# Moving every operand of the float32r matmuls to one place modulo 512 bytes

## The chip, the cores and the metric

The kernel runs on one core of a Trainium2 chip. The metric is the device time of one launch in microseconds (us), taken as the median of several runs. A core has TensorE (PE in the profile, its loads of stationary operands as PEld), VectorE (DVE), ScalarE (ACT), GpSimd (POOL) and SyncE (SP), which work side by side on an on-chip memory of 128 partitions; TensorE writes its sums into a second, smaller memory, PSUM. An operand's address below is its byte offset inside a partition, the same in all 128, and its *place* is that address modulo 512.

## The reference

One layer of a hybrid decoder on 1024 tokens of width 2048, all in float32: an RMS norm, one input projection to 8200 columns, two recurrences on its parts, an output projection, a gated per-layer input, a last norm.

```python
u = rmsnorm(h, norm_w[l])
proj = einsum('bsd,dc->bsc', u, w_in[l])
...
h_a = mlstm_chunkwise(q_a, k_a, v_a, i_pre, f_pre)
y_a = sigmoid(ml_o) * rmsnorm(h_a) * silu(ml_z)
h_b = hgrn2_chunkwise(q_b, k_b, logf_b, i_b)
y_b = rmsnorm(h_b) * silu(hg_g)
h = h + einsum('bsc,cd->bsd', concat([y_a, y_b]), w_out[l])
e = einsum('bsr,rd->bsd', p[l], w_pe[l])
gate = sigmoid(einsum('bsd,de->bse', rmsnorm(h, pe_norm_w[l]), w_pg[l]))
out = rmsnorm(h + gate * e, final_norm_w)
```

## The kernel before

The four large products (input projection, output projection, gate, per-layer input) are float32 products made of three float32r passes. Each operand is split into a rounded *high* part and the exact remainder, the *low* part (`split`, L113 to L115: a cast on ScalarE, then a subtraction on VectorE). The helper `mm3` then issues three matmuls into one PSUM bank: high by high (L242), high by low (L243), low by high (L244). A matmul has a *stationary* operand of 128x128, which a load (LDWEIGHTS in the trace) brings into the array, and a *moving* operand of 128 rows by 512, 264 or 256 columns that streams past it.

Tokens are handled in two halves of 512. First part, for each half: `prep_u` makes 16 split tiles `u` of the normed input; `proj_ch` (outputs `pj`) takes slices of the weights `hl` as stationary and `u` as moving operand, 512 columns wide; `proj_tok` (outputs `pt`) has it the other way round, `u` stationary and `hl` moving, 256 columns wide (264 in one block a half, the one that carries the gates). Between these stand the recurrences, whose matmuls are plain float32, apart from `col_sums` (L514, L515), which multiplies a stationary tile of ones, `ones_r`, by split products. Second part, for each half: output projection (outputs `po`, stationary `ys`, the split mixed heads; moving `hl_o`), then the gate (outputs `pg`, stationary `hnt`; moving `hl_g`) and the per-layer input (outputs `pe`, stationary `pp`; moving `hl_e`). All have 512 columns but the last token tile of all (`bg`), which has two groups of 256.

Weights come in pieces of 128x1024 float32, three pieces ahead, by DMAs on SP's queue into `raw` (pool `wpool`, three buffers) and are split into `hl`, also three buffers. A `hl` tile has two planes, high and low, of WP = 1056 columns each. The order of the instructions is made by a scheduler when the kernel is built; GpSimd writes `y` and `h` to DRAM and is otherwise nearly idle.

Where a tile lies in a partition follows from the order in which the pools are opened and from their sizes. Before, the runtime's DMA scratch (16,384 bytes) and 128 bytes of small constants come first, then `const`, `upool`, `stage`, `wpool`, `small`, `mix`; `tl` takes `mix`'s room in the second part. `upool` starts at 19,360 = 37 x 512 + 416, and a `u` tile has 4,096 bytes, so every `u` and `ys` plane has place 416. A `hl` buffer has 8,448 = 16.5 x 512 bytes and a plane 4,224 = 8.25 x 512, so places alternate between buffers.

| operand (pool) | place before | place after |
|---|---|---|
| `u`, `ys`, high and low (`upool`) | 416 | 128 |
| `hl`, high plane, three buffers | 288, 32, 288 | 128 |
| `hl`, low plane, three buffers | 416, 160, 416 | 128 |
| `hnt` and `pp` (`tl`) | 448 | 128 |
| `ones_r` | 96 | 128 |
| split products of `col_sums` (`mix`) | 448 | 128 |

In the 264-column block the slices of `hl` are 1,056 bytes apart, so there the place of the moving operand advances by 32 bytes from slice to slice, before and after.

Of the kernel before, what the change touches and what calls it, by code (L numbers as in the profile page):

```python
"""Hybrid decoder layer (mLSTM heads and HGRN2 heads side by side) on one core.

Tokens are handled in two halves. The projections run as float32 products split
into three float32r passes (each operand is the sum of a rounded part and an exact
remainder), channels on the output partitions, so that both recurrences find their
queries and keys transposed. The recurrences work in chunks of 128 tokens; HGRN2's
decays are formed as products over blocks of doubling size, so no factor exceeds one.
"""
# [9 lines left out]
F32R = mybir.dt.float32r  # L18
# [6 lines left out]
P = 128  # L25
# [6 lines left out]
AHEAD = 3  # L32
WP = 1056
BIG = 1e30
LEVELS = (4, 8, 16, 32, 64)
# [8 lines left out]
def hybrid_layer(ctx: ExitStack, tc, x, xT, pT, w_blk, w_v0, w_out, w_pg, w_pe, vec, gb, fnw,  # L44
                 ident_in, causal_in, lmask_in, out):
    nc = tc.nc
    PS = bass.MemoryType.PSUM

    const = ctx.enter_context(tc.tile_pool(name="const", bufs=1))
    upool = ctx.enter_context(tc.tile_pool(name="upool", bufs=17))  # L50
    stage = ctx.enter_context(tc.tile_pool(name="stage", bufs=3))
    wpool = ctx.enter_context(tc.tile_pool(name="wpool", bufs=3))
# [13 lines left out]

# [1 line left out]
    vec_sb = const.tile([P, V_END], F32, name="vec_sb")  # L68
# [10 lines left out]
    nc.vector.memset(ones, 1.0)  # L79
    ones_r = const.tile([P, P], F32R, name="ones_r")  # L80
    nc.scalar.copy(out=ones_r, in_=ones)

    # lower bound: softmax over the two rows, first row
    lb = const.tile([P, 8], F32, name="lb")
# [12 lines left out]

    # states carried between halves
    mcar = const.tile([4, 1], F32, name="mcar")
# [11 lines left out]

# [1 line left out]
    def split(dst_hi, dst_lo, src):  # L113
# [8 lines left out]

    # weights arrive as [P, 1024] slices in the order of use, some slices ahead
    w_order, w_tiles = [], []
# [15 lines left out]
    def next_piece(between=None):  # L140
        nm, src = w_order[len(w_tiles)]
        n = src.shape[1] * src.shape[2]
        raw = wpool.tile([P, WP], F32, tag="wraw", name=f"raw_{nm}")[:, 0:n]
        if nm in LATE:
            hl = [upool.tile([P, 2, HT], F32R, tag="u", name=f"hl_{nm}_{i}") for i in range(2)]
            nc.sync.dma_start(out=raw, in_=src.rearrange("p k c -> p (k c)"))
            for i in range(2):
                split(hl[i][:, 0], hl[i][:, 1], raw[:, i * 512:(i + 1) * 512])
            w_tiles.append((nm, hl))
            return  # L150
        hl = wpool.tile([P, 2, WP], F32R, tag="whl", name=f"hl_{nm}")[:, :, 0:n]
        parts = 4 if not w_tiles else 1
        for i in range(parts):
            k0, k1 = i * src.shape[1] // parts, (i + 1) * src.shape[1] // parts
            sl = slice(k0 * src.shape[2], k1 * src.shape[2])
            nc.sync.dma_start(out=raw[:, sl], in_=src[:, k0:k1].rearrange("p k c -> p (k c)"))
            if between is not None:
                between(i)
            split(hl[:, 0, sl], hl[:, 1, sl], raw[:, sl])
        w_tiles.append((nm, hl))  # L160

    def load_piece(name):
        """the next slice of weights, split: [P, 2, n]"""
        while len(w_tiles) < len(w_order) and (len(w_tiles) < AHEAD or w_order[len(w_tiles) - AHEAD][0] != name):
            next_piece()
        return dict(w_tiles[-AHEAD - 4:])[name]

    def prep_stats(half):
        """1 / rms of the tokens: as columns [P, chunk] and as a row on every partition"""
        ss = small.tile([P, NC, 4], F32, tag="ssx", name=f"ssx{half}")  # L170
# [27 lines left out]
    def prep_u(half):  # L198
        """x^T times the norm weight, split; 1 / rms is applied to the projections"""
        us = []  # L200
# [45 lines left out]
    def proj_ch(half, us, b):  # L246
        """two column tiles of the block, channels on partitions: two banks [P, 512]"""
        ps = [psj(f"pj{half}_{b}_{i}") for i in range(2)]
        for pc in range(4):
            hl = load_piece(f"{half}_{b}_{pc}")  # L250
            for kk in range(4):
                k = pc * 4 + kk
                for i in range(2):
                    sl = slice(kk * 256 + i * P, kk * 256 + (i + 1) * P)
                    mm3(ps[i], hl[:, 0, sl], hl[:, 1, sl], us[k][:, 0], us[k][:, 1], k == 0, k == KT - 1)
        return ps

    def proj_tok(half, us, b, n=256):
        """the block with tokens on partitions: four banks [P, n]"""
        ps = [psj(f"pt{half}_{b}_{i}") for i in range(NC)]  # L260
# [10 lines left out]

# [1 line left out]
    def gates(half, pv, rc):  # L273
        """pv: banks with the gates' input and forget parts in columns 256-259 and 260-263"""
        gp = small.tile([P, NC, 8], F32, tag="gp", name=f"gp{half}")
# [13 lines left out]
        nc.scalar.activation(out=fp, in_=prow[1][0:4, :], func=AF.Identity, bias=gb_sb[:, 1:2])  # L289
        # log sigmoid(f) = min(f, 0) - log1p(exp(-|f|)), log1p(e) = 2 atanh(e / (2 + e))  # L290
        nc.vector.scalar_tensor_tensor(out=t1, in0=fp, scalar=-1.0, in1=fp, op0=ALU.mult, op1=ALU.max)
# [6 lines left out]
        for n in (15, 13, 11, 9, 7, 5, 3):  # L298
# [3 lines left out]
        nc.vector.scalar_tensor_tensor(out=fp, in0=t3, scalar=-2.0, in1=fp, op0=ALU.mult, op1=ALU.add)  # L302
        # cumulative log forget inside a chunk, running maximum
        nc.vector.tensor_tensor_scan(out=b_, data0=rst, data1=fp, initial=0.0, op0=ALU.mult, op1=ALU.add)
# [17 lines left out]
                                in1=alast.unsqueeze(2).broadcast_to([4, NC, P]), op=ALU.add)  # L322
        # columns: beta, floor exp(-m), state weight
        stk = mix.tile([P, HT], F32, tag="y", bufs=2, name=f"stk{half}")[0:68]
# [8 lines left out]
        nc.vector.tensor_copy(out=cols, in_=pc[:, 0:NC * 68].rearrange("p (c r) -> p c r", r=68))  # L333
        # rows, broadcast over partitions through DRAM
        rows = tc.dram_tile([4, 2, HT], F32, name=f"rows{half}")
# [4 lines left out]

# [1 line left out]
    def mlstm_unit(half, us, hd, rs, gc):  # L342
        n = f"{half}_{hd}"
# [57 lines left out]

        # decays and weighted scores, keys on partitions
        dq = mix.tile([P, 2 * NC, P], F32, tag="at", bufs=1, name=f"dq{n}")
# [58 lines left out]

# [1 line left out]
    def hgrn_unit(half, us, pr, rs):  # L464
# [35 lines left out]

        # scores within a chunk: the diagonal, then pairs of blocks of doubling size
        qf = q.rearrange("p a b -> p (a b)")
# [4 lines left out]
        def col_sums(prod, name):  # L507
            """sums over the partitions of [P, 512] products, on every partition"""
            tag = ("kh", "sg")[spl[0] % 2]
# [7 lines left out]

        # pairs inside a block of four tokens: elementwise products, summed over the state dimension
        ff = f.rearrange("p a b -> p (a b)")
# [41 lines left out]
        toff = HT + 256  # L561
        # pairs of blocks of doubling size
        for li, s in enumerate(LEVELS):
# [24 lines left out]
            toff += nblk  # L588
        # T: product of the forget gates over each chunk
        kh = mix.tile([P, H2, P], F32, tag="kh", bufs=1, name=f"hkh{n}")  # L590
# [54 lines left out]

# [1 line left out]
    rs = None  # L647
# [13 lines left out]

# [1 line left out]
    tl = ctx.enter_context(tc.tile_pool(name="tl", bufs=1, reuse_waits="tile"))  # L663
    for half in range(2):
# [53 lines left out]
        def gate_block(cb, ts_, pref):  # L718
            """gate and per-layer input for the token tiles ts_ of one block of 512 columns"""
            cs = slice(cb * 512, (cb + 1) * 512)  # L720
            wpe = load_piece(f"{pref}e{half}_{cb}")
            pe_sb = {}
            for t in ts_:
# [5 lines left out]
                pe_sb[t] = pe  # L729
            # the last tile of all comes in two groups of columns, to shorten what follows its products  # L730
            units = []
# [138 lines left out]
```

## Time and profile before

| | |
|---|---|
| time, median of 3 runs | 2429.19 us (2429.04 to 2430.67) |
| span of the profiled execution | 2427.2 us |
| instructions | 30,855 |
| TensorE busy | 2410.4 us, 99% of the span |
| VectorE busy | 1166.3 us, 48% |
| ScalarE busy | 767.8 us, 32% |
| DMA | 287.57 MB, mean 118 GB/s |

The span goes from the first to the last instruction of one execution that the profiler recorded; that execution has no other time of its own, and its span is 2.0 us under the median of the runs. A matmul's recorded duration runs to the end of its pipeline, and that end is modelled, so that consecutive matmuls overlap in a list by time. What a matmul costs is the *step*: the distance from its start to the start of the next one.

### The profile page before, as it was taken

The numbers are of one execution on the slowest core, as the hardware profiler recorded it, in microseconds if no ns is written. First come the engines' busy times: TensorE is split into PE (matmuls) and PEld (weight loads), VectorE is DVE, ScalarE is ACT, GpSimd is POOL, SyncE is SP. The second block draws the span as 40 slices with busy tenths as digits, with TensorE's granted clock in tenths as the row PEclk, the third lists the DMA queues.
The fourth block names the chain that finished last, engine by engine and source line by source line (L and its number), as shares of the span: only waits on it lengthen the run. The fifth ranks groups of instructions, "written<-read, shape, count | busy, mean of one in ns | idle before, by whom it ended". The sixth has DMA issues, their size and how long they took to land.

```text
span 2427.2 us, 30855 instructions
## 1 busy us (share of the span) xinstructions
PE 2410.4 (99%) x12700; PEld 2044.1 (84%) x12700; DVE 1166.3 (48%) x1657; ACT 767.8 (32%) x1211; POOL 66.3 (3%) x96
## 2 busy tenths in 40 slices
PE   8999999999999999999999999999999999999998
PEld 7888889888888888888888888888888888888887
DVE  6655344355564847344246364565423444332336
ACT  6433232223222424223222222242322334332225
POOL 0000000000000000000000000000000000000000
PEclk9999999999999999999999999999999999999999
DMA  8433332222222423333332222243444446444336
GB/s 315 136 97 103 94 100 94 91 78 93 79 87 81 156 78 105 96 108 101 94 107 87 87 79 89 78 150 122 135 130 127 132 146 222 135 154 130 117 114 212
DMA packets 93461, 287.57 MB, mean 118 GB/s; under 512 B 10872, under 2 KB 11640, under 8 KB 93320
## 3 DMA queue, kind: packets, MB, share of 16 engines
q1 hardware_dynamic: 88200, 268.82, 35.0%
q0 software_dynamic: 5120, 16.78, 1.8%
q8 instruction: 99, 1.62, 0.3%
q14 instruction: 42, 0.34, 0.0%
HBM read 260.36 MB, written 25.20 MB: 118 GB/s over the span
## 4 chain that ended last, share of the span: by engine, by line
PE 98%; DMA 0%; issue 0%; DVE 0%; ACT 0%; SPq 0%; POOL 0%; POOLq 0%; ACTq 0%; DVEq 0%
PE pj L244 15%; PE pj L243 15%; PE pj L242 15%; PE pg L242 5%; PE pt L242 5%; PE pg L244 5%; PE pt L244 5%; PE pg L243 5%; PE po L242 5%; PE pt L243 5%; PE po L244 5%; PE po L243 5%; PE pl L570 2%; PE pe L242 1%; PE pe L244 1%; PE pe L243 1%
## 5 line engine op out<-in xcount | busy, mean ns | idle before, releaser
L242 PE MATMUL pj<-u,hl 128*128 128x512 f32 x1536 | 608.0, 399 | 5.9 <-ACT hl L114 5.9
L244 PE MATMUL pj<-u,hl 128*128 128x512 f32 x1536 | 611.3, 399 | 0.0
L243 PE MATMUL pj<-u,hl 128*128 128x512 f32 x1536 | 610.8, 398 | 0.2 <-DVE u L230 0.2
L114 ACT CAST hl<-raw 128x1024 fp32r<-128x1024 f32 (+2 forms) x259 | 269.2, 1040 | 863.1 <-PE pj L244 449.1
L115 DVE TENSOR_TENSOR hl<-raw,hl 128x1024 fp32r<-128x1024 f32 (+2 forms) x259 | 313.5, 1211 | 402.4 <-ACT hl L114 402.2
L242 PEld LDWEIGHTS pj<-u,hl 128*128 128x128 f32 x1536 | 289.1, 188 | 72.6 <-ACT hl L114 5.9
L243 PEld LDWEIGHTS pj<-u,hl 128*128 128x128 f32 x1536 | 289.4, 188 | 70.0 <-DVE u L230 1.1
L244 PEld LDWEIGHTS pj<-u,hl 128*128 128x128 f32 x1536 | 289.1, 188 | 66.7 <-issue 0.2
L242 PE MATMUL pt<-hl,u 128*128 128x256 f32 (+1 forms) x1024 | 291.1, 285 | 0.4 <-DVE raw L357 0.4
L244 PE MATMUL pt<-hl,u 128*128 128x256 f32 (+1 forms) x1024 | 290.2, 285 | 0.0
L243 PE MATMUL pt<-hl,u 128*128 128x256 f32 (+1 forms) x1024 | 288.8, 283 | 0.0
L242 PE MATMUL po<-hl_o,ys 128*128 128x512 f32 x512 | 202.1, 395 | 0.0
L244 PE MATMUL po<-hl_o,ys 128*128 128x512 f32 x512 | 200.3, 392 | 0.0
L243 PE MATMUL po<-hl_o,ys 128*128 128x512 f32 x512 | 199.8, 390 | 0.0
L242 PEld LDWEIGHTS pt<-hl,u 128*128 128x128 f32 x1024 | 193.7, 189 | 2.2 <-issue 1.1
L243 PEld LDWEIGHTS pt<-hl,u 128*128 128x128 f32 x1024 | 194.0, 189 | 1.3
L244 PEld LDWEIGHTS pt<-hl,u 128*128 128x128 f32 x1024 | 192.4, 188 | 0.9 <-issue 0.2
L242 PE MATMUL pg<-hl_g,hnt 128*128 128x512 f32 x448 | 177.9, 397 | 0.0
L244 PE MATMUL pg<-hl_g,hnt 128*128 128x512 f32 x448 | 177.9, 397 | 0.0
L243 PE MATMUL pg<-hl_g,hnt 128*128 128x512 f32 x448 | 177.1, 395 | 0.0
L115 DVE TENSOR_TENSOR hl_o<-raw_o,hl_o 128x1024 fp32r<-128x1024 f32 x64 | 78.4, 1225 | 161.9 <-ACT hl_o L114 161.9
L115 DVE TENSOR_TENSOR hl_g<-raw_g,hl_g 128x1024 fp32r<-128x1024 f32 x56 | 68.6, 1225 | 174.5 <-ACT hl_g L114 174.5
(264 smaller groups left out, 2642.9 us busy)
## 6 DMA issues: line engine op xcount, KB each, us to landing
raw<-in_w_blk_dram SPq DMA_DIRECT2D x247, 512.0 KB, 3.9
raw_o<-in_w_out_dram SPq DMA_DIRECT2D x64, 512.0 KB, 3.6
raw_g<-in_w_pg_dram SPq DMA_DIRECT2D x56, 512.0 KB, 3.7
yr<-y SPq DMA_DIRECT2D x32, 256.0 KB, 4.0
xr<-in_x_dram SPq DMA_DIRECT2D x32, 256.0 KB, 5.7
h<-ht POOLq DMA_DIRECT2D x32, 256.0 KB, 6.3
hr<-h SPq DMA_DIRECT2D x32, 256.0 KB, 3.6
out_dram<-h SPq DMA_DIRECT2D x32, 256.0 KB, 3.5
```

What stands on the lines that cost most here:

```text
L114: nc.scalar.copy(out=dst_hi, in_=src)
L115: nc.vector.tensor_tensor(out=dst_lo, in0=src, in1=dst_hi.bitcast(F32), op=ALU.subtract)
L242: nc.tensor.matmul(ps, lhsT=ah, rhs=bh, start=first, stop=False)
L243: nc.tensor.matmul(ps, lhsT=ah, rhs=bl, start=False, stop=False)
L244: nc.tensor.matmul(ps, lhsT=al, rhs=bh, start=False, stop=last)
L570: nc.tensor.matmul(pl[0:M, c * 64:(c + 1) * 64], lhsT=kf[:, c * P:c * P + M], rhs=qv[:, c * nb:(c + 1) * nb, 1, :], start=True, stop=True)
```

## The change

The diff without its removed comment lines and docstrings (line numbers behind the helpers grow by four):

```diff
+WH = 1152
...
-    const = ctx.enter_context(tc.tile_pool(name="const", bufs=1))
     upool = ctx.enter_context(tc.tile_pool(name="upool", bufs=17))
+    hlpool = ctx.enter_context(tc.tile_pool(name="hlpool", bufs=3))
+    orpool = ctx.enter_context(tc.tile_pool(name="orpool", bufs=1))
     stage = ctx.enter_context(tc.tile_pool(name="stage", bufs=3))
+    const = ctx.enter_context(tc.tile_pool(name="const", bufs=1))
     wpool = ctx.enter_context(tc.tile_pool(name="wpool", bufs=3))
...
-    ones_r = const.tile([P, P], F32R, name="ones_r")
+    ones_r = orpool.tile([P, P + 112], F32R, name="ones_r")[:, 0:P]
...
-        hl = wpool.tile([P, 2, WP], F32R, tag="whl", name=f"hl_{nm}")[:, :, 0:n]
+        hl = hlpool.tile([P, 2, WH], F32R, tag="whl", name=f"hl_{nm}")[:, :, 0:n]
...
-    nc = _bacc.Bacc("TRN2", target_bir_lowering=False, num_devices=1)
+    nc = _bacc.Bacc("TRN2", target_bir_lowering=False, num_devices=1, dynamic_dma_scratch_size=8192)
```

`upool` comes first, behind a DMA scratch of half the size, and starts at 8,320 = 16 x 512 + 128. The split weights have a pool of their own right behind it, with planes of 1152 columns = 9 x 512 bytes. `ones_r` follows, with 112 columns of padding behind it that nothing reads; the padding sets where `mix`, and with it `tl`, begins: 129,152 = 252 x 512 + 128. The table above has the places that result. On every engine the built program has the same instructions on the same operands in the same order as before, and the same waits; only the addresses differ.

## Rows read from the trace of the kernel before

**Rows 1.** The page: busy time, share of the span and count by engine; the granted TensorE clock in 40 slices (tenths of full speed); the chain of work that ended last, by engine.

```profile
PE 2410.4 (99%) x12700; PEld 2044.1 (84%) x12700; DVE 1166.3 (48%) x1657; ACT 767.8 (32%) x1211; POOL 66.3 (3%) x96
...
PEclk9999999999999999999999999999999999999999
...
PE 98%; DMA 0%; issue 0%; DVE 0%; ACT 0%; SPq 0%; POOL 0%; POOLq 0%; ACTq 0%; DVEq 0%
```

**Rows 2.** What TensorE waited for: us in total, times, longest.

```profile
PE pj L242 <- ACT hl L114: 5.9, 1, 5.9
PE prow L282 <- DVE gp L277: 1.0, 1, 1.0
```

**Rows 3.** Groups of TensorE's instructions by line and shape: output and operands, rows and columns, count, busy us and mean ns of one, idle before.

```profile
L244 PE MATMUL pj<-u,hl 128*128 128x512 f32 x1536 | 611.3, 399 | 0.0
L243 PE MATMUL pj<-u,hl 128*128 128x512 f32 x1536 | 610.8, 398 | 0.2 <-DVE u L230 0.2
L242 PE MATMUL pj<-u,hl 128*128 128x512 f32 x1536 | 608.0, 399 | 5.9 <-ACT hl L114 5.9
L242 PE MATMUL pt<-hl,u 128*128 128x256 f32 x896 | 254.8, 285 | 0.0
...
L243 PE MATMUL pt<-hl,u 128*128 128x256 f32 x896 | 252.3, 282 | 0.0
L242 PE MATMUL po<-hl_o,ys 128*128 128x512 f32 x512 | 202.1, 395 | 0.0
L244 PE MATMUL po<-hl_o,ys 128*128 128x512 f32 x512 | 200.3, 392 | 0.0
L243 PE MATMUL po<-hl_o,ys 128*128 128x512 f32 x512 | 199.8, 390 | 0.0
L242 PE MATMUL pg<-hl_g,hnt 128*128 128x512 f32 x448 | 177.9, 397 | 0.0
L244 PE MATMUL pg<-hl_g,hnt 128*128 128x512 f32 x448 | 177.9, 397 | 0.0
L243 PE MATMUL pg<-hl_g,hnt 128*128 128x512 f32 x448 | 177.1, 395 | 0.0
...
L244 PE MATMUL pe<-hl_e,pp 128*128 128x512 f32 x56 | 22.2, 397 | 0.0
...
L244 PE MATMUL pg<-hl_ag,hnt 128*128 128x512 f32 x32 | 12.7, 397 | 0.0
...
L243 PE MATMUL pg<-hl_bg,hnt 128*128 128x512 f32 x16 | 6.3, 395 | 0.0
```

**Rows 4.** Instructions of TensorE in order of time in the input projection, `pj`: start us, duration us, line, operands. From the first row to the last are 12 steps.

```profile
799.65 0.40 PE L244 MATMUL pj<-u,hl 128*128 128x512 f32 x1
799.89 0.39 PE L242 MATMUL pj<-u,hl 128*128 128x512 f32 x1
800.12 0.40 PE L243 MATMUL pj<-u,hl 128*128 128x512 f32 x1
...
802.45 0.40 PE L244 MATMUL pj<-u,hl 128*128 128x512 f32 x1
```

**Rows 5.** The same in the output projection, `po`; 12 steps from the first row to the last.

```profile
1759.63 0.39 PE L244 MATMUL po<-hl_o,ys 128*128 128x512 f32 x1
...
1762.38 0.39 PE L244 MATMUL po<-hl_o,ys 128*128 128x512 f32 x1
```

**Rows 6.** The same in the gate, `pg`; 12 steps from the first row to the last.

```profile
1899.78 0.40 PE L244 MATMUL pg<-hl_g,hnt 128*128 128x512 f32 x1
...
1902.58 0.40 PE L244 MATMUL pg<-hl_g,hnt 128*128 128x512 f32 x1
```

**Rows 7.** The same in a block with 256 columns, `pt`; 24 steps from the first row to the last.

```profile
1181.91 0.28 PE L244 MATMUL pt<-hl,u 128*128 128x256 f32 x1
...
1184.80 0.28 PE L244 MATMUL pt<-hl,u 128*128 128x256 f32 x1
```

**Rows 8.** Matmuls and loads of stationary operands together, in order of time, in the output projection: the load that a matmul of one line needs carries that line.

```profile
1760.10 0.39 PE L243 MATMUL po<-hl_o,ys 128*128 128x512 f32 x1
1760.10 0.19 PEld L244 LDWEIGHTS po<-hl_o,ys 128*128 128x128 f32 x1
1760.32 0.39 PE L244 MATMUL po<-hl_o,ys 128*128 128x512 f32 x1
1760.32 0.19 PEld L242 LDWEIGHTS po<-hl_o,ys 128*128 128x128 f32 x1
```

**Rows 9.** Groups by line: the two instructions that split a piece of weights of the input projection (count, busy us and mean ns of one, idle before and what ended it).

```profile
L115 DVE TENSOR_TENSOR hl<-raw,hl 128x1024 fp32r<-128x1024 f32 (+2 forms) x259 | 313.5, 1211 | 402.4 <-ACT hl L114 402.2
...
L114 ACT CAST hl<-raw 128x1024 fp32r<-128x1024 f32 (+2 forms) x259 | 269.2, 1040 | 863.1 <-PE pj L244 449.1 <-PE pt L244 162.6 <-issue 84.4
```

**Rows 10.** DMA issues by line: queue, count, KB each, median us from issue to landing.

```profile
raw<-in_w_blk_dram SPq DMA_DIRECT2D x247, 512.0 KB, 3.9
...
h<-ht POOLq DMA_DIRECT2D x32, 256.0 KB, 6.3
...
y<-hy POOLq DMA_DIRECT2D x16, 256.0 KB, 3.2
```

More of the change, by code (lines that the diff above doesn't have):

```diff
@@ L47, in hybrid_layer @@
     PS = bass.MemoryType.PSUM
+    upool = ctx.enter_context(tc.tile_pool(name="upool", bufs=17))
+    hlpool = ctx.enter_context(tc.tile_pool(name="hlpool", bufs=3))
+    orpool = ctx.enter_context(tc.tile_pool(name="orpool", bufs=1))
+    stage = ctx.enter_context(tc.tile_pool(name="stage", bufs=3))
     const = ctx.enter_context(tc.tile_pool(name="const", bufs=1))
-    upool = ctx.enter_context(tc.tile_pool(name="upool", bufs=17))
-    stage = ctx.enter_context(tc.tile_pool(name="stage", bufs=3))
     wpool = ctx.enter_context(tc.tile_pool(name="wpool", bufs=3))
```

## The prediction

> **What bounds the kernel now.** I read the page first. TensorE is busy 99% of the span, the chain of work that ended last lies on it for 98%, and the granted clock stands in the top tenth in all 40 slices [rows 1]: the upper of its two levels, 2.4 GHz, throughout. The list of waits comes next, since a busy engine may hide short stalls: the longest is 5.9 us, at the start, and the next is 1.0 us [rows 2]. So no transfer, no split and no other engine sets the time; what a change can win or lose is the time that TensorE takes from one matmul to the next. The change moves no instruction, so only that step can differ.
>
> The third view is therefore TensorE's instructions in order of time, of which the reader is to take the distance between starts, not the durations. In the input projection 12 steps take 802.45 - 799.65 = 2.80 us, 233.3 ns each [rows 4]; in the output projection 2.75 us, 229.2 ns [rows 5]; in the gate 2.80 us, 233.3 ns [rows 6]. All have 128x128 stationary and 512 moving columns, at the same clock, and none waits. The two in the second part differ in nearly nothing: the same helper, the same order of the three passes, moving operands in the same buffers. What differs is the stationary operand: `ys` at place 416 in the output projection, `hnt` at 448 in the gate. Against moving operands at 288, 416, 32 and 160, the first is a multiple of 128 bytes away, the second never is. Between two such neighbours 4.2 ns a matmul go with 32 bytes. The grouped view says the same in durations: 395, 392 and 390 ns in the output projection, 397, 397 and 395 in the gate [rows 3].
>
> The input projection warns against the simplest reading. Its moving `u` at 416 and stationary `hl` at 288, 32, 416 and 160 are also multiples of 128 apart, and it still steps 233.3 ns. Its difference from the output projection is that its stationary operand changes place from pass to pass while the moving one stays. So I can't say which relation counts, only that the one loop whose loads all lie at one place, a multiple of 128 from what streams, is the fast one.
>
> A fourth view shows why places could matter at all: the load for the next matmul starts at the same hundredth of a microsecond as the matmul before it [rows 8], so in every step two streams start to read the same partitions together.
>
> **The change part by part.** It removes and adds no instruction; the padding and the wider planes are never read or written. Three parts could cost or gain.
>
> First, the places of the 512-column products. Afterwards stationary and moving operand, this pass and the next, all lie at 128: no distance and no change of place. The fast loop is the nearest row, so I take its step for all. The products that now step 233.3 ns are 3 x 1536 in the input projection, 3 x 448 + 3 x 32 + 3 x 16 in the gate and 3 x 56 in the per-layer input (397 ns there, as in the gate) [rows 3]: 4608 + 1488 + 168 = 6264. At 233.3 - 229.2 = 4.2 ns each they give 26.1 us. The 1536 products of the output projection I leave at 229.2 ns.
>
> Neither end of this term is shown, since no matmul here has all its operands at one place. The lower end comes from comparing widths. A 256-column matmul steps 2.89 us / 24 = 120.4 ns [rows 7], so the last 256 columns of the output projection cost 229.2 - 120.4 = 108.8 ns, and 512 columns with nothing else would cost 217.6. If every surcharge went: 6264 x 15.7 = 98 us, 1536 x 11.6 = 18 us, 2688 products of 256 columns x 11.6 = 31 us, in all 147 us, and 2282 us. The upper end I set as a mirror image, an estimate: if equal places were as bad as they may be good, each of the 6264 goes up by 4.2 ns and each of the 1536 by 8.4, which adds 26 + 13 = 39 us and gives 2468. I take the fast loop's step because it is the nearest measured case, not the middle of these ends.
>
> Second, the 256-column products (3 x 896 [rows 3]): their stationary `u` is at 416 already and the moving operands a multiple of 128 away, as in the output projection. I cost them at nothing; the bounds above hold them too.
>
> Third, the smaller DMA scratch and whatever moved beside the products. GpSimd issues the writes of `h` and `y`, which land 6.3 and 3.2 us after issue [rows 10] and are read again only in a later stage; GpSimd is busy 3% [rows 1]. I cost it at nothing: TensorE's work until the next stage hides it, and with that cover gone one late write of 6.3 us at the change of part would be the price. The splits keep pace: a piece feeds 24 matmuls of the input projection, 24 x 229.2 = 5.5 us, against 1.04 us on ScalarE and 1.21 us on VectorE [rows 9] and 3.9 us for the transfer [rows 10], three pieces ahead. Nothing is late next; TensorE stays the bound.
>
> The sum: 2429.2 - 26.1 = 2403.1. I worked it out in the profiled execution, whose span of 2427.2 us lies 2.0 us under the median; by the span it would be 2401.1, and I add the 2.0 back.
>
> **The rivals.** *A deeper gain.* In the output projection the pass with the low moving plane, L243, is the shortest of all at 390 ns [rows 3]; in two of three buffers its two operands are both at 416. If equal places are what shortens it and all passes come down to 390, the input projection's mean of 398.7 loses 8.7 x 4608 = 40 us, gate and per-layer input 6.3 x 1656 = 10 us, the output projection 2.3 x 1536 = 4 us; with 1 ns on the 256-column products, about 57 us and 2372. Against it: duration ends are modelled, and in the input projection the pass whose two operands are at 416 in two of three buffers, L244, has 399 ns and is not short.
>
> *Nothing.* The loads may not meet the streams at all, and the 4.2 ns belong to something else in the second part. For it speaks that input projection and gate step alike, although their distances differ. It gives 2429.
> The Trainium skill, "TensorE: Matmul & The Clock Gate", section "Part 2: What happens when you issue a matmul", speaks for this rival: TensorE has two independent read ports, and loading the next weights takes no read bandwidth from the running matmul. By that rule places would not matter and the time would stay at 2429; the trace's 233.3 against 229.2 ns in two loops that differ in one place doesn't agree with the rule as it stands, which is why this rival gets a small chance.
>
> *Slower.* What makes the output projection fast is not the relation of the operands but that its stationary operand starts at 416 itself; at 128, as at 448 in the gate, the advantage goes. The place of the price is the output projection, 1536 x 4.2 = 6.5 us, and, if their loads lose as much, the 2688 products of 256 columns, another 11.3 us: 2436 to 2447, while input projection and gate stay at 233.3. For it: only one fast place is known, and no row shows 128. Against it: the input projection has 416 among its stationary places (every low plane of two buffers) and gains nothing on L244. It decides as soon as 12 steps of the output projection take 2.80 us where they took 2.75.
>
> **How the numbers follow.** The forecast, with its neighbourhood of about 2385 to 2415, gets 0.42, the deeper gain 0.23, nothing 0.12, slower 0.23. A measurement of this kernel tells about 0.2% from no change, 4.9 us; the forecast (-26) and the deeper gain (-57) lie beyond it and make faster 0.65, same 0.12; the slower rival begins at +6.5 and holds all of slower, 0.23. The predicted time is 2403. The range reaches over the deeper gain half way to the lower end, 2345, because a fast case that no row shows may go beyond the 390 ns, and up to 2445, nearly all of the slower rival; I leave about 1 in 10 out on each side.
>
> **What would show it.** In the changed profile 12 steps of input projection and gate should take 2.75 us as in [rows 5], and those of the output projection no more than that; the grouped durations of the three should agree with each other within 1 or 2 ns, since all have the same places now. Counts, waits and the busy times of VectorE and ScalarE should stay as they are. If the three agree at 2.80 us, the slower rival holds; if they agree well below 2.75, the deeper gain does; if gate and output projection still differ by 4 ns, place was never the cause. A wait of TensorE over a few microseconds behind a split or a transfer would mean that the new places harm something I took to be covered.

## The result and the profile after

The changed kernel takes 2389.08 us (median of 5 runs, 2388.27 to 2389.55) where the kernel before takes 2429.19 (2428.86 to 2430.67): a ratio of 0.9835, 95% interval 0.9823 to 0.9847, 40.1 us less. The forecast was 2403.

The page of the changed kernel, in the order of [rows 1]: busy time and counts by engine, granted clock, chain by engine.

```profile
PE 2370.0 (99%) x12700; PEld 2043.5 (86%) x12700; DVE 1165.5 (49%) x1657; ACT 766.2 (32%) x1211; POOL 66.5 (3%) x96
...
PEclk9999999999999999999999999999999999999999
...
PE 98%; DMA 0%; issue 0%; DVE 0%; ACT 0%; SPq 0%; POOL 0%; POOLq 0%; ACTq 0%; DVEq 0%
```

Same counts, same clock, same chain. TensorE's busy time falls by 40.4 us and with it the span, by 40.0; VectorE and ScalarE move by 1 us or 2. The waits of TensorE (us in total, times, longest) are those of [rows 2]:

```profile
PE pj L246 <- ACT hl L118: 5.8, 1, 5.8
PE prow L286 <- DVE gp L281: 1.0, 1, 1.0
```

So the whole gain is in the step. TensorE in order of time, for [rows 4, 5, 6]: input projection, output projection and gate; in each, 12 steps from the first row to the last:

```profile
779.74 0.39 PE L248 MATMUL pj<-u,hl 128*128 128x512 f32 x1
779.97 0.39 PE L246 MATMUL pj<-u,hl 128*128 128x512 f32 x1
780.20 0.39 PE L247 MATMUL pj<-u,hl 128*128 128x512 f32 x1
...
782.46 0.39 PE L248 MATMUL pj<-u,hl 128*128 128x512 f32 x1
...
1719.77 0.39 PE L248 MATMUL po<-hl_o,ys 128*128 128x512 f32 x1
...
1722.49 0.39 PE L248 MATMUL po<-hl_o,ys 128*128 128x512 f32 x1
...
1869.72 0.39 PE L248 MATMUL pg<-hl_g,hnt 128*128 128x512 f32 x1
...
1872.44 0.39 PE L248 MATMUL pg<-hl_g,hnt 128*128 128x512 f32 x1
```

12 steps take 2.72 us in all three, 226.7 ns, where the input projection and the gate had 233.3 [rows 4, 6] and the output projection 229.2 [rows 5]. The reader is to take two things from these rows: the three loops now agree to the hundredth, and they agree below the fastest loop of before. The products of 256 columns did not follow; 24 steps, for [rows 7]:

```profile
1164.92 0.28 PE L248 MATMUL pt<-hl,u 128*128 128x256 f32 x1
...
1167.80 0.28 PE L248 MATMUL pt<-hl,u 128*128 128x256 f32 x1
```

2.88 us, 120.0 ns; before it was 120.4 in the stretch of [rows 7]. The groups by line and shape, for [rows 3]:

```profile
L247 PE MATMUL pj<-u,hl 128*128 128x512 f32 x1536 | 602.5, 392 | 0.2 <-DVE u L234 0.2
L246 PE MATMUL pj<-u,hl 128*128 128x512 f32 x1536 | 602.1, 395 | 6.5 <-ACT hl L118 5.8 <-ACT u L233 0.7
L248 PE MATMUL pj<-u,hl 128*128 128x512 f32 x1536 | 600.2, 391 | 0.0
L246 PE MATMUL pt<-hl,u 128*128 128x256 f32 x896 | 254.2, 285 | 0.0
...
L246 PE MATMUL po<-hl_o,ys 128*128 128x512 f32 x512 | 200.4, 392 | 0.0
L247 PE MATMUL po<-hl_o,ys 128*128 128x512 f32 x512 | 200.2, 391 | 0.0
L248 PE MATMUL po<-hl_o,ys 128*128 128x512 f32 x512 | 199.4, 390 | 0.0
L246 PE MATMUL pg<-hl_g,hnt 128*128 128x512 f32 x448 | 174.9, 390 | 0.0
L247 PE MATMUL pg<-hl_g,hnt 128*128 128x512 f32 x448 | 174.5, 390 | 0.0
L248 PE MATMUL pg<-hl_g,hnt 128*128 128x512 f32 x448 | 174.3, 389 | 0.0
```

The three loops agree less closely in these durations than in steps: 392.7, 391.0 and 389.7 ns on average. Since durations overlap, the busy times of these lines can't be added up to say where the gain comes from. The steps can: over all matmuls of a product in the two traces, each from its start to the start of TensorE's next matmul, they sum to 1091.6 us before and 1065.2 after in the input projection, 26.4 less; in the gate (512 columns) 347.9 and 338.4, 9.5 less; in the output projection 354.4 and 351.5, 2.9 less; in the per-layer input 44.8 and 43.5, 1.3 less; in the products of 256 columns 325.2 and 326.2, 1.0 more. All steps of the trace together fall by 39.8 us.

### The profile page after: what moved, and what is told of

Same layout as the page of the kernel before. It is cut to its first block, busy times and chain, and to the rows that moved or that the text cites. A ratio compares the mean times of both kernels' runs of the same rounds, so it can differ in the third digit from the quotient of the medians.

```text
span 2387.2 us, 30855 instructions
## 1 busy us (share of the span) xinstructions
PE 2370.0 (99%) x12700; PEld 2043.5 (86%) x12700; DVE 1165.5 (49%) x1657; ACT 766.2 (32%) x1211; POOL 66.5 (3%) x96
## 4 chain that ended last, share of the span: by engine, by line
PE 98%; DMA 0%; issue 0%; DVE 0%; ACT 0%; SPq 0%; POOL 0%; POOLq 0%; ACTq 0%; DVEq 0%
PE pj L246 15%; PE pj L247 15%; PE pj L248 15%; PE pt L246 5%; PE pt L247 5%; PE pt L248 5%; PE po L246 5%; PE pg L247 5%; PE pg L248 5%; PE po L247 5%; PE po L248 5%; PE pg L246 5%; PE pl L574 2%; PE pe L246 1%; PE pe L248 1%; PE pe L247 1%
## 5 line engine op out<-in xcount | busy, mean ns | idle before, releaser
L246 PE MATMUL pj<-u,hl 128*128 128x512 f32 x1536 | 602.1, 395 | 6.5 <-ACT hl L118 5.8
L247 PE MATMUL pj<-u,hl 128*128 128x512 f32 x1536 | 602.5, 392 | 0.2 <-DVE u L234 0.2
L248 PE MATMUL pj<-u,hl 128*128 128x512 f32 x1536 | 600.2, 391 | 0.0
L246 PEld LDWEIGHTS pt<-hl,u 128*128 128x128 f32 x1024 | 195.4, 191 | 2.1 <-issue 1.1
L247 PEld LDWEIGHTS pt<-hl,u 128*128 128x128 f32 x1024 | 195.7, 191 | 1.2
L248 PEld LDWEIGHTS pt<-hl,u 128*128 128x128 f32 x1024 | 195.0, 191 | 0.9 <-issue 0.2
L246 PE MATMUL pg<-hl_g,hnt 128*128 128x512 f32 x448 | 174.9, 390 | 0.0
L247 PE MATMUL pg<-hl_g,hnt 128*128 128x512 f32 x448 | 174.5, 390 | 0.0
L248 PE MATMUL pg<-hl_g,hnt 128*128 128x512 f32 x448 | 174.3, 389 | 0.0
```

The source lines that it names most:

```text
L246: nc.tensor.matmul(ps, lhsT=ah, rhs=bh, start=first, stop=False)
L247: nc.tensor.matmul(ps, lhsT=ah, rhs=bl, start=False, stop=False)
L248: nc.tensor.matmul(ps, lhsT=al, rhs=bh, start=False, stop=last)
```

## The experiments

Steps are given as the median, over all pieces of weights in a trace, of three consecutive steps (the three passes) divided by three; "distance" is the place of the stationary operand less that of the moving one of the same matmul. Every kernel runs the full computation. Times stand beside runs of the kernel before on the same chip, medians of 2429.10 to 2429.32 us.

**Which part: relation or place.** Theory R says that the relation of the operands counts, theory A each operand's own place, theory S the smaller DMA scratch. In `all_at_160`, 32 bytes precede `upool` (the memset that touches them is one short instruction of VectorE more):

```diff
+    gappool = ctx.enter_context(tc.tile_pool(name="gappool", bufs=1))
+    gap = gappool.tile([P, 8], F32, name="gap")
+    nc.vector.memset(gap[:, 0:1], 0.0)
     upool = ctx.enter_context(tc.tile_pool(name="upool", bufs=17))
```

> The changed kernel with 32 bytes put in front, so that every float32r operand lies at place 160 instead of 128; the distances between operands stay zero. Theory R (only the relation of the operands counts): nothing changes, 2389 us within 3, 512-column steps 226.7 ns. Theory A (each operand's own place counts; 128 is a multiple of 64 bytes, 160 and all places of the input and output projection before are 32 past one): the steps go back to between 229 and 233 ns, 7800 x 2.5 to 6.6 ns = 20 to 50 us, so 2409 to 2439 us.

Measured: 2388.77 us, ratio to before 0.9835 (0.9820 to 0.9850), the input projection's 12 steps as in the changed kernel:

```profile
998.18 0.39 PE L251 MATMUL pj<-u,hl 128*128 128x512 f32 x1
...
1000.90 0.39 PE L251 MATMUL pj<-u,hl 128*128 128x512 f32 x1
```

2.72 us at place 160 as at 128. A falls: 32 bytes more on every operand change nothing, R stands.

`before_small_scratch` is the kernel before with only the scratch changed:

```diff
-    nc = _bacc.Bacc("TRN2", target_bir_lowering=False, num_devices=1)
+    nc = _bacc.Bacc("TRN2", target_bir_lowering=False, num_devices=1, dynamic_dma_scratch_size=8192)
```

> The kernel before with the smaller DMA scratch alone; all addresses fall by 8192, so no place modulo 512 changes. Theories R and A: 2429 us, all steps as before. Theory S (the smaller scratch, or the lower addresses, carry part of the gain): between 2389 and 2425 us. If the scratch harms GpSimd's writes: above 2431 us.

Measured: 2428.75 us, ratio 0.9998 (0.9989 to 1.0008). S falls: the time with the smaller scratch is that of the kernel before within 0.1%.

`before_tl_at_416` tests the pair of loops on which the prediction rested. To the kernel before with the small scratch it adds 480 bytes in front of `mix` and `tl`, so that the gate's stationary `hnt` lies at 416, like `ys` of the output projection:

```diff
+    gappool = ctx.enter_context(tc.tile_pool(name="gappool", bufs=1))
+    gap = gappool.tile([P, 120], F32, name="gap")
+    nc.vector.memset(gap[:, 0:1], 0.0)
```

> The kernel before, with the smaller DMA scratch and 480 bytes put in front of the pools mix and tl: hnt, pp and the products of col_sums lie at 416 instead of 448, all else as before. Theory R: gate and per-layer input get the step of the output projection, 229.2 ns, 1656 x 4.2 = 7 us less: 2422 us; input and output projection stay at 233.3 and 229.2. Theory A (multiples of 64 bytes are good): 448 was the better place, the gate gets no faster, 2429 us or above. Theory N (something else in the second part makes the gate slower than the output projection): 2429 us.

Measured: 2422.07 us, ratio 0.9972 (0.9961 to 0.9983). 12 steps of the gate:

```profile
2008.57 0.39 PE L246 MATMUL pg<-hl_g,hnt 128*128 128x512 f32 x1
...
2011.32 0.39 PE L246 MATMUL pg<-hl_g,hnt 128*128 128x512 f32 x1
```

2.75 us: the gate has the step of [rows 5] as soon as it has its places (57 of its 63 pieces of weights step 229 ns, where before 60 stepped 233), and the kernel takes 7 us less, as computed. A change of place alone removes the difference between these two loops. That equal places always mean equal steps isn't shown; the next kernel speaks against it.

**Undoing the wide planes.** `planes_of_1056` is the changed kernel with

```diff
-WH = 1152
+WH = 1056
-    ones_r = orpool.tile([P, P + 112], F32R, name="ones_r")[:, 0:P]
+    ones_r = orpool.tile([P, P + 176], F32R, name="ones_r")[:, 0:P]
```

> The changed kernel with the planes of the split weights 1056 columns wide again (and the padding behind ones_r enlarged so that hnt and pp stay at 128): high planes of the three buffers at 128, 384, 128, low planes at 256, 0, 256; everything else at 128. Theory R with a modulus of 512 or 256: the input projection, whose loaded operand changes place from pass to pass, goes back to 233.3 ns (4608 x 6.6 = +30 us), output projection, gate and per-layer input to 229.2 (3200 x 2.5 = +8 us): about 2427 us. Theory A, or a relation modulo 128: 2389 us, steps 226.7 ns.

Measured: 2414.01 us, ratio 0.9940 (0.9923 to 0.9956). Input projection 231.0 ns, output projection 233.3, gate mostly 229.0 and partly 233.3. A relation modulo 128 falls, for all distances here are multiples of 128. R has the direction, but its sizes were off: the input projection lost less than the 30 us given, the output projection more. The two kinds of buffer (high planes at 128 and at 384) step alike, a first sign that 256 is a period.

One thing in this kernel goes against a rule by places alone. `ys` and `hnt` both lie at 128, and the moving operands have the same buffers, so output projection and gate have the same distances. Yet of 64 pieces of weights of the output projection 45 step 233 ns and 13 step 229, and of 63 pieces of the gate 14 step 233 and 43 step 229. The gate shows both in one trace, first in one piece, then in another of the same buffer, 12 steps each:

```profile
1864.22 0.40 PE L247 MATMUL pg<-hl_g,hnt 128*128 128x512 f32 x1
...
1867.02 0.40 PE L247 MATMUL pg<-hl_g,hnt 128*128 128x512 f32 x1
...
1880.93 0.40 PE L247 MATMUL pg<-hl_g,hnt 128*128 128x512 f32 x1
...
1883.68 0.40 PE L247 MATMUL pg<-hl_g,hnt 128*128 128x512 f32 x1
```

2.80 us and 2.75 us at the same places. Between the two, matmuls of other products broke into the stream. So the steps here have two patterns, and what breaks in can move the loop from one to the other; it then stays there until the next interruption, in the output projection up to 178 steps long. In the changed kernel the loop comes back instead: a step of about 315 ns, where other matmuls broke in, is followed by some of up to 236 ns, and after at most nine of them the steps of the output projection are at 227 again, if nothing else breaks in before. Why is not shown.

**Constant distances.** In three kernels the three buffers of `hl` get tiles of unequal size, so that both planes of a buffer lie at one place and each buffer at another; the pieces go round the buffers, so each trace holds three distances side by side. The core of the edit:

```diff
-        hl = hlpool.tile([P, 2, WH], F32R, tag="whl", name=f"hl_{nm}")[:, :, 0:n]
+        b = hl_count[0] % 3
+        hl_count[0] += 1
+        hl = hlpool.tile([P, HLS[b]], F32R, tag=f"whl{b}", name=f"hl_{nm}")
+        hl = hl[:, 0:2 * WH].rearrange("p (a c) -> p a c", a=2)[:, :, 0:n]
```

> The changed kernel with the three buffers of split weights at places 160, 192 and 224 (both planes of a buffer alike), u and ys at 128, hnt and pp at 32: in each piece of weights the distance of the loaded from the streaming operand is constant and not zero. Input projection: +32, +64, +96 by buffer; output projection: -32, -64, -96; gate: -128, -160, -192. Theory R0 (only equal places are fast): every 512-column step about 233 ns, 7800 x 6.6 = +52 us, 2440 us. Theory R128 (multiples of 128 are as good as equal): the same but for the gate's pieces at -128, 226.7 there, 2437 us. Theory C (what costs is the change of distance from pass to pass, not the distance): 226.7 ns everywhere, 2389 us.

> The mirror image: buffers of split weights at 96, 64 and 32, u and ys at 128, hnt and pp at 224. Input projection: -32, -64, -96; output projection +32, +64, +96; gate +128, +160, +192. Theory R0: 2440 us. R128: 2437 us. C: 2389 us. If it matters which of the two streams is ahead, this kernel and its mirror image differ.

> The changed kernel with the buffers of split weights at 352, 384 and 416, all else at 128: distances of 224, 256 and 288 in all loops. Theory R0 with a modulus of 512: 2440 us, all steps about 233 ns. R0 with a modulus of 256, or R128: the pieces of the middle buffer step 226.7 ns, those of the other two 233: 2424 us. C: 2389 us.

Measured: 2430.95, 2424.71 and 2417.54 us (ratios 1.0008, 0.9981, 0.9954). Theory C falls: a constant distance other than zero is slow. The third kernel has the plainest picture, TensorE in the input projection in a piece at distance 224 and, a microsecond later, in one at 256; 12 steps each:

```profile
1029.97 0.39 PE L254 MATMUL pj<-u,hl 128*128 128x512 f32 x1
...
1032.77 0.39 PE L254 MATMUL pj<-u,hl 128*128 128x512 f32 x1
...
1033.69 0.39 PE L255 MATMUL pj<-u,hl 128*128 128x512 f32 x1
...
1036.41 0.39 PE L255 MATMUL pj<-u,hl 128*128 128x512 f32 x1
```

2.80 us and 2.72 us: 256 is as good as zero, so for these places the period is 256 bytes, not 512. Over the three kernels, as medians:

| distance modulo 256 | 512 columns, step | 256 columns, step |
|---|---|---|
| 0 | 226.7 ns | 120.0 ns |
| 192 | 229.0 | 117.7 |
| 128 | 231.7 (gate alone) | |
| 32, 64, 96, 160, 224 | 232.7 to 234.3 | 117.0 to 119.3 |

Two entries hide two patterns: at 128 the triples of steps lie near 230 or near 235 ns, and at 192 in the input projection 752 of 1298 lie at 229 and 433 at 233.

The totals lie below those that R0 gave, 2440 and, for the third, 2424: by 9 and 15 us in the first two kernels and by 6.5 in the third. One reason stands in the last column: of these distances the narrow products are slowest at equal places and gain where the wide ones lose, a point that no theory had.

**Finer steps.** `fine_distances` shifts the weights of each piece inside their tile; the core of the edit (`kind` names the product, and `v` is the block with the gates):

```diff
-        hl = hlpool.tile([P, 2, WH], F32R, tag="whl", name=f"hl_{nm}")[:, :, 0:n]
+        o = count.get(kind, 0) % 64 if kind != "v" else 0
+        count[kind] = count.get(kind, 0) + 1
+        hl = hlpool.tile([P, 2, WH], F32R, tag="whl", name=f"hl_{nm}")[:, :, o:o + n]
```

> The changed kernel with the split weights of each piece shifted inside their tile by a number of float32 that goes up by one from piece to piece (0, 4, 8, ... 252 bytes, counted apart for the input projection with 512 columns, the products of 256 columns, the output projection and the gate): 64 distances in one run. Both planes of a piece are shifted alike. Coarse theory: only distances within 16 bytes of a multiple of 256 step 226.7 ns with 512 columns, some near 192 step 229 and all others 231 to 234.3; none is under 226.7. Fine theory: there is a distance that the runs in steps of 32 bytes missed, with steps under 226. In all about 2425 us by the coarse theory, since most pieces have a bad distance for 512 columns.

Measured, in a single run: 2429.81 us beside 2429.26 for the kernel before. No distance steps clearly under 226.7 ns with 512 columns, so the fine theory has nothing for it. The coarse theory isn't confirmed either: some distances that are no multiples of 16 (in output projection and gate 100, 148, 196 and 228) step 226.7 to 227.0, others (12, 60, 124, 252) up to 240. With one or two pieces for a distance, and moving operands that begin off multiples of 16 bytes, the run can't fully separate the two causes. Two things can be read from it. In the input projection the moving operand stays at 128, and there the pieces at 120, 132, 244 and 252 have a median of 226.7 too, so equal places are not the only fast ones. In output projection and gate, distances 4 past a multiple of 16 average 229.6 and 229.9 ns, those 12 past it 235.9 and 237.2; in the input projection it is not so (234.3 and 232.9), which points to where the moving operand begins. A single piece is a weak witness for wide products: the only one of the output projection at equal places stepped 230.2 here, where the changed kernel has 226.7. For 256 columns it named one distance, 144, with a mean of 114.9 ns over a single piece.

**Apart for the narrow products.** The products of 256 columns have pieces of their own, so their weights alone can be shifted, by `o` = 48, 28 or 7 float32, which puts the two operands at distances 64, 144 and 228 modulo 256. The core of the first:

```diff
-        hl = hlpool.tile([P, 2, WH], F32R, tag="whl", name=f"hl_{nm}")[:, :, 0:n]
+        b = int(nm.split("_")[1]) if nm[0].isdigit() else -1
+        o = 48 if b >= 0 and b != 2 and b % 4 == (2 if b < 16 else 0) else 0
+        hl = hlpool.tile([P, 2, WH], F32R, tag="whl", name=f"hl_{nm}")[:, :, o:o + n]
```

> The changed kernel with the split weights of the 256-column products alone shifted by 192 bytes in their tiles: u stays at 128, the moving weights lie at 320, a distance of 64 modulo 256, while all 512-column products keep equal places. In the runs before, equal places gave 120.5 ns on average with 256 columns and this distance 117.3. Theory: 2688 x 3.2 = 8.5 us less than the changed kernel, 2380.6 us. If the two widths have the same rule and the 117.3 was an effect of something else: 2389 us or above.

> As narrow_apart, but with a shift of 112 bytes for the weights of the 256-column products: moving operand at 240, distance 144 modulo 256, the one with the shortest mean step (114.9 ns, in a single piece) among 56 distances of fine_distances. If the piece told the truth: 2688 x (117.4 - 114.9) = 6.7 us less than narrow_apart, 2374 us. If it was chance, and distance 64 is as good as it gets: 2381 us.

> The same with a shift of 28 bytes: moving operand at 156, distance 228, 115.9 ns in a single piece of fine_distances; 28 is no multiple of 16. If the piece told the truth: 2688 x 1.5 = 4 us less than narrow_apart, 2377 us; if 512-column products with moving operands off multiples of 16 (up to 240 ns there) are a warning for 256 columns too: above 2381 us.

Measured: 2380.92, 2374.21 and 2378.42 us (ratios to before 0.9801, 0.9778 and 0.9794, the second with the interval 0.9762 to 0.9794). The first and the third gain 8.2 and 10.7 us on the changed kernel. For 228, 2378.42 lies near the 2377 expected if the piece told the truth. The single piece told the truth about 144: this version is 14.9 us faster than the changed kernel, and its 256-column steps sum to 6.6 us less than those of `narrow_apart`, where 6.7 was expected. 24 steps of it:

```profile
1052.60 0.28 PE L248 MATMUL pt<-hl,u 128*128 128x256 f32 x1
...
1055.32 0.28 PE L248 MATMUL pt<-hl,u 128*128 128x256 f32 x1
```

2.72 us, 113.3 ns each, against 2.88 us in the changed kernel. It is the fastest version of this study.

**Which two streams.** In [rows 8] the load for the next matmul starts together with the matmul before it. Two relations are therefore possible: a moving operand with the load that runs beside it (theory L), or with its own stationary operand (theory O). With both planes alike they are the same. `low_planes_at_160` puts all low planes 32 bytes on, with high and low planes of `u` and `ys` in pools of their own; the core of the edit:

```diff
-WH = 1152
+WH = 1160
-    upool = ctx.enter_context(tc.tile_pool(name="upool", bufs=17))
+    uhpool = ctx.enter_context(tc.tile_pool(name="uhpool", bufs=17))
+    gap1 = ctx.enter_context(tc.tile_pool(name="gap1", bufs=1)).tile([P, 8], F32, name="gap1")
+    ulpool = ctx.enter_context(tc.tile_pool(name="ulpool", bufs=17))
+    gap2 = ctx.enter_context(tc.tile_pool(name="gap2", bufs=1)).tile([P, 120], F32, name="gap2")
```

> The changed kernel with the low planes of u, ys and hl all at 160 and the high planes at 128; hnt and pp keep both planes at 128. In input and output projection and in the 256-column products, the load that runs beside each matmul (that of the next one) then still has the place of the operand that streams, while the matmul's own two operands are 32 bytes apart in two passes of three. In gate and per-layer input both are 32 bytes apart in L243's counterpart alone. Theory L (the load that runs beside the stream counts): input and output projection step 226.7 ns as in the changed kernel, gate and per-layer input somewhat more, by up to 6.6 x 1656 = 11 us: 2389 to 2400 us. Theory O (a matmul's own two operands count): input and output projection step 229 to 233 ns, 6144 x 2.3 to 6.6 = 14 to 41 us, and the gate 4 to 11 us more: 2407 to 2441 us.

Measured: 2427.77 us, ratio 0.9996 (0.9987 to 1.0006). Input projection, 12 steps:

```profile
1005.82 0.39 PE L262 MATMUL pj<-u_l,hl 128*128 128x512 f32 x1
...
1008.60 0.39 PE L262 MATMUL pj<-u_l,hl 128*128 128x512 f32 x1
```

2.78 us, 231.7 ns, although each load beside a matmul still has its place: L isn't enough. O's range held. But O isn't shown to be the rule either: the gate, where one pass of three is 32 bytes apart, steps 231.3 ns, nearly as much as the input projection with two of three, so a sum over passes, each by its own distance, doesn't give these steps. About 7 us of this kernel's time are not due to places. With planes in separate tiles the scheduler ordered some passes differently, and the waits of TensorE have two new rows; behind the longer one the granted clock is lower. The waits, then the window behind the first of them (start and end, length, TensorE's busy time and matmuls, granted clock, share of the DMA engines, GB/s):

```profile
PE po L263 <- DVE ys_l L133: 3.7, 1, 3.7
...
PE po L261 <- ACT ys_h L132: 0.8, 1, 0.8
...
2028.70:2034.50 5.80, 5.79 (x14) 0.50 0.93 336
```

A granted clock of 0.50 is the lower of the two levels, 1.2 GHz: after TensorE had stood idle for 3.7 us, 12 steps took 427 ns each, where the output projection's median here is 232. Waits and slow steps come to 3.7 + 0.8 + 12 x 0.195 = 6.8 us; without them the kernel would take about 2421 us, an estimate, which is still in O's range.

## Why the prediction was right, and where its size was off

*TensorE's step alone can differ.* Right: span and TensorE's busy time fall by the same 40 us, with waits, counts and clock as before.

*Places matter, and output projection against gate shows it.* Right, and shown by the run that moved `hnt` and `pp`: 7 us for 1656 products, as computed. (The products of `col_sums` moved with them, and the smaller scratch, shown to do nothing, was in it.)

*The 6264 products get the step of the fast loop, 26.1 us.* The term that was mis-sized. Their step became 226.7 ns, not 229.2, so with 6.6 ns each the term is 41 us. By the sums of steps 37.2 of it arrived (26.4, 9.5 and 1.3 in input projection, gate and per-layer input). The input projection got 5.7 ns a product, where 4608 x 6.6 would be 30 us, because not every product stands in a regular sequence: in the changed trace 608 of its 4608 steps still take 229 ns or more, but only 225 of the 3973 that stand in the regular order of the passes.

*The output projection stays at 229.2 ns.* Wrong by 2.5 ns a step, 2.9 us in the sum of steps: of its three passes one (L243) had a distance of 0 modulo 256 and two had 128, so its places were not the best. I took the nearest measured case where the best one was not among the rows.

*The 256-column products at nothing.* Right in the sum of steps, 325.2 us before and 326.2 after, but by luck: places change their step as well (113.3 ns at a distance of 144), and those of before happened to cost about the same as equal places.

*Scratch and cover at nothing.* Right, shown for the scratch by its own run; no new wait of TensorE appears.

*Durations of the three loops within 1 or 2 ns.* Not quite: 392.7, 391.0 and 389.7 ns, a spread of 3, with steps that agree.

The rivals: *slower* falls by the result: with its stationary operand at 128 the output projection takes 2.72 us for 12 steps, not 2.80, and in `all_at_160` 160 does as well, so 416 had no merit of its own. *Nothing* falls, since the step went from 233.3 to 226.7 ns: the places of the two operands relative to each other count. The Trainium skill, "TensorE: Matmul & The Clock Gate", section "Part 2: What happens when you issue a matmul", says that TensorE's two read ports are independent. By what I drew from that the step would have stayed at 233.3 ns, with which these runs don't agree. *A deeper gain* described the durations well (389 to 395 ns in all three loops) and the time too low, 2372 for 2389, mostly because the input projection's mean duration came down to 392.7 ns and not to 390: its steps gave 26.4 us where the rival had 40. The 256-column products, for which it had 3 us, gave none. The truth lies between it and the forecast. Why the input projection was slow although its distances were multiples of 128 is answered in part: 128 steps 231.7 ns in the gate even when constant, and a mix of distances from pass to pass is slow too, as in `planes_of_1056`. What a mix costs I can't compute: modulo 256 the input projection of before had the same distances from pass to pass as the output projection, 128, 128 and 0, only with the 0 in L244 and not in L243, and stepped 233.3 ns against 229.2. How the places act on the step stays open.

## What to carry to other kernels

In a stream of float32r matmuls that keeps TensorE at 99%, measure starts, not durations, and compare loops of equal shape: a difference of 2% between two of them is worth a run that moves one operand by 32 bytes. Put stationary and moving operands of 512-column products at one address modulo 256, all planes alike, by pool order and padding; for narrower products try distances in a few pieces of one run first, since there equal places were slower than many. Check a candidate in a full run: a loop can keep a slower pattern after an interruption at the same places.

## What was not expected

The period is 256 bytes, as far as distances of 0 and 256 show it. No distance tried is clearly better than equal places for 512 columns (226.7 ns against up to 234.3 in steps of 32 bytes), and for 256 columns many are (120.0 ns against 113.3 at a distance of 144). A loop with the same operands' places can run in either of two patterns, 229 or 233 ns in `planes_of_1056`. And a sweep in which each piece of weights has its own distance gave, in one run, a candidate that a full run then confirmed to within 1 us: 2374 expected, 2374.21 measured. That a single piece is enough to find one isn't shown: for the wide products it wasn't.
